# A diffusion layer on one core: first stage without GpSimd, DRAM sums filled later, modulations spread one by one, broadcasts moved up

## The chip, the cores and the metric

The kernel runs on one core of a Trainium2 chip. Times are microseconds (us) on the device. Five engines work side by side and meet through semaphores: TensorE (PE in the profile; its weight loads are PEld), VectorE (DVE), ScalarE (ACT), GpSimd (POOL) and SyncE (SP, which here only issues DMAs). ACT and POOL issue DMAs as well.

## The reference

One layer on 512 latent tokens x and 256 context tokens ctx, width 1024, all in float32. Nine modulation vectors come from c (for x) and from c_ctx (for ctx).

```python
h = h + 0.5 * g1 * swiglu(modulate(h, norm_ffn1, sh1, sc1), w_ffn1_in, w_ffn1_out)
hc = hc + 0.5 * g1c * swiglu(modulate(hc, norm_ffn1, sh1c, sc1c), w_ffn1_in, w_ffn1_out)
u, uc = modulate(h, norm_mix, sh2, sc2), modulate(hc, norm_mix, sh2c, sc2c)
kv_c = uc @ w_in[:, K0:G0]                       # the context gives only keys and values
q, k, v, rg, cv, ga, gb = split(u @ w_in)
o = bidir_retention(rope(q), rope(k), v, context states)
h = h + g2 * ((sigmoid(ga) * retention_out(o, rg) + sigmoid(gb) * conv_branch(cv)) @ w_out)
h = h + 0.5 * g3 * swiglu(modulate(h, norm_ffn2, sh3, sc3), w_ffn2_in, w_ffn2_out)
return rmsnorm(h, final_norm)

def modulate(x, w, shift, scale):
    return x * rsqrt(mean(x * x) + EPS) * w * (1 + scale) + shift
def swiglu(x, w_in, w_out):
    a, b = split(x @ w_in)
    return (silu(a) * b) @ w_out
# mods = split(silu(c) @ w_mod + b_mod, 9): sh1, sc1, g1, sh2, sc2, g2, sh3, sc3, g3
```

## The kernel before

Channels lie on the 128 partitions in eight blocks (KT = 8), tokens along the free dimension: 0 to 511 are x (`xs`), 512 to 767 ctx (`cx`). Each float32 operand is split into a high and a low part, `hi` (ScalarE, a rounding copy) and `lo` (VectorE, a subtraction), and each product is three matmuls (`mm3`: hi by hi, lo by hi, hi by lo). Weights come in units of 512 KB: a DMA on SP's queue into one of four `wraw` buffers, then `wh` on ScalarE and `wl` on VectorE.

The order of the instructions on each engine is made at build time by a list scheduler, from the program's order and from which buffers are free (6 `t`, 4 `sg`, 2 `wm`, 8 PSUM banks `ps`). At run time each engine goes through its list in order and waits at each instruction for what it needs. DMAs wait in the same way in the list of the engine that issues them.

- **First stage** (`start`, `first_mods`, `shift`, `norm_start`). x is loaded, its squares are summed over channels (`square_sum`, then `rstd_sum` with matmuls against ones), and 1/rms is broadcast over the partitions with one more matmul (`rstd_bcast`). For each block b, `first_mods` computes that block's scale and shift for x and ctx at once: the scale by eight small matmuls with `cs` (columns of silu(c), silu(c_ctx)), a copy of the two rows and a transpose; the shift by dots of the weight tile with the broadcast rows `ccrow`, for x on VectorE (L183), for ctx by a multiply on GpSimd (L186) and a sum on ScalarE (L187). `shift` adds the two halves and the bias (L194, L195). `norm_start` makes the block's operand (L530 to L533), and `products` runs the first two pairs of weight units of FFN1 on the blocks that are done. Then the context is done the same way, its matmuls after all products of x.
- **hdram** holds x and ctx in DRAM; FFN1's partial sums are added to it by accumulating DMAs (`part_sum`) and read back at the end.
- **FFN1** runs in six groups of hidden blocks; from the second on each block is a `chunk` (a seven-product scheme on four-block halves). The 56 other modulation tiles are loaded by GpSimd into `wm` (L200) and reduced by VectorE (L206), a few after each chunk or output pair (`mod_step(count)`).
- **Handover to the mixers** (`tail1`, `head2`, `retention(0)`, `keys_c`, `rotated`). FFN1's last outputs come in two halves of the tokens. Each half has its rstd sum, broadcast and norms; between them stand the context's keys. `rotated` makes keys and queries, `roped` turns them (L733 to L736), `strips` makes the decay tables with exp, `conv_at` a chunk of the convolution branch.

Of the kernel before, what the change touches and what calls it, by code (L numbers as in the profile page):

```python
# [54 lines left out]


# [6 lines left out]
def hybrid_layer_kernel(ctx: ExitStack, tc: tile.TileContext, a: dict, out: bass.AP):  # L63
# [62 lines left out]
    nc.sync.dma_start(cs, a["ccT"])  # L126
# [38 lines left out]
    rtags = [f"{t}{i}" for i in range(8) for t in ("th", "tl")]  # L165

    def first_mods(b):


        raw = [[t_((P, 512), F32, rtags[(4 * b + 2 * i + n) % 16]) for n in range(2)] for i in range(2)]  # L170
        for i in range(2):
            for n in range(2):
                nc.sync.dma_start(raw[i][n], a["w_mod0"][2 * b + i, :, n * 512:(n + 1) * 512])
        pm = ps()
        for k in range(KT):
            nc.tensor.matmul(pm[0:2, 0:P], cs[:, k, :], raw[0][k // 4][:, k % 4 * P:(k % 4 + 1) * P],
                             start=k == 0, stop=k == KT - 1)
        row = tmp()
        nc.vector.tensor_copy(row[0:2, 0:P], pm[0:2, 0:P])
        nc.tensor.transpose(pm[:, P:P + 2], row[0:2, 0:P], ident[0:2, 0:2])  # L180
        for n in range(2):
            c = slice(n * 512, (n + 1) * 512)
            nc.vector.scalar_tensor_tensor(tmp((P, 512), BF16), raw[1][n], 1.0, ccrow[0][:, c], ALU.mult, ALU.mult,  # L183
                                           accum_out=dots[:, b, 0, n:n + 1])
# [3 lines left out]
        nc.vector.tensor_scalar(ab1[:, 0, b, :], pm[:, P:P + 2], bm1[:, 8 + b:9 + b], vec[:, V_N1 + b:V_N1 + b + 1],  # L188
                                ALU.add, ALU.mult)
        shift(slice(b, b + 1), 0)  # L190

    def shift(bs, v):
        t = ab1[:, 1, bs, v]
        nc.vector.tensor_add(t, dots[:, bs, v, 0], dots[:, bs, v, 1])  # L194
        nc.vector.tensor_add(t, t, vec[:, V_BM + bs.start:V_BM + bs.stop])  # L195
# [183 lines left out]
    def chunk(j, u, t, keep):  # L379
# [34 lines left out]
        nc.scalar.activation(s[:, lo_], pa, AF.Silu)  # L414
        product(pd, w1, 1, [x[3] for x in t], False)
# [20 lines left out]
    def ffn1(u):  # L436
# [7 lines left out]
        def plain(pa, pb, pc):  # L444
            s = t_((P, LA), F32, "sg", 4)
            nc.scalar.activation(s[:, xs], pa, AF.Silu)
            nc.vector.tensor_mul(s[:, xs], s[:, xs], pb)
            nc.scalar.activation(s[:, cx], pc[:, 0, :], AF.Silu)
            nc.vector.tensor_mul(s[:, cx], s[:, cx], pc[:, 1, :])
            return s  # L450

        ux, uc = part(u, xs), part(u, cx)
        todo_g = [plain(*p) for p in start(ux, uc)]
# [4 lines left out]
        for gi, (k0, nk) in enumerate(GROUPS1):  # L458
            for j in range(2 if k0 == 0 else 0, nk):
                if k0 and j == nk - 1:  # L460
                    g.append((t_((P, LA), F32R, f"hx{2 * j}"), t_((P, LA), F32R, f"hx{2 * j + 1}")))
                    chunk(k0 + j, u, t, lambda s, c: split(g[-1][0][:, c], g[-1][1][:, c], s[:, c]))
                elif k0:
                    keep(j, chunk(k0 + j, u, t, None))
# [9 lines left out]
                keep(j, plain(pa, pb, pc))  # L474
# [9 lines left out]

            for mm in () if last else range(4):
                mod_step(STEPS_OUT[gi] * (mm + 1) // 4 - STEPS_OUT[gi] * mm // 4)
# [6 lines left out]
                for i in range(2):  # L493
                    part_sum(2 * mm + i, px[i], pc[i][:, :LC])
# [40 lines left out]
    def start(u, uc):  # L535
# [7 lines left out]
        r1 = r1c = None  # L543
# [8 lines left out]
        dg = rstd_sum(acc, sq, whole)  # L552
        for b in range(KT):
            first_mods(b)
            if b == 0:
                r1 = rstd_bcast(dg)
                w += units(a["w1i"][0])
# [3 lines left out]
            if b == 5:  # L561
                for i in range(KT):
                    nc.sync.dma_start(hx[i][:, cx], a["ctxT"][:, i, :])
# [5 lines left out]
        products(0, 7)  # L569
# [75 lines left out]
    def tail1(n, h, hc):  # L645
# [118 lines left out]
    def retention(hd):  # L764
# [35 lines left out]
        if hd == 0:  # L800
# [284 lines left out]
def _layout(x, c, ctx, c_ctx, w_mod, b_mod, norm_ffn1, w_ffn1_in, w_ffn1_out, norm_mix, w_in, ret_decay_f,  # L1085
# [15 lines left out]
    def out_groups(w, groups):  # L1101
# [3 lines left out]
    wn = w_mod[0][:, D:2 * D].reshape(KT, P, 8, P).transpose(2, 1, 0, 3).reshape(8, P, -1)  # L1105
# [16 lines left out]
        "w_mod0": np.stack([w for b in range(8) for w in (wn[b], wm[0, b])]),  # L1122
# [37 lines left out]
```

## Time and profile before

| | |
|---|---|
| median of three runs | 1781.86 us (1779.5 to 1781.98) |
| profiled execution | 1779.1 us |
| its span | 1777.0 us |
| mean granted TensorE clock | 0.985 |
| busy in the span: PE, DVE, ACT, POOL | 1723.9, 1150.4, 676.0, 141.6 us |

The span runs from the first to the last instruction that the profiler records; the execution's time adds what lies around it. "PE busy" counts matmuls at whatever clock was granted. In a row of waits, the first name is what stood still and the second what it waited for, by the line of each. In a row of the timeline the first number is the start in us, the second the length, and the bracket at the end the idle time before it with its releaser.

### The profile page before, as it was taken

How to read it: one execution, taken by the hardware profiler on the slowest of the kernel's cores; microseconds unless marked ns; L12 is line 12 of the kernel's file. 1: busy time of each engine (PE TensorE's matmuls, PEld its weight loads, DVE VectorE, ACT ScalarE, POOL GpSimd, SP SyncE). 2: the span in 40 equal slices, each digit the busy share in tenths (PEclk: the TensorE clock that was granted, in tenths of full speed). 3: DMA queues.
4: the chain of work that ended last, by engine and by line, in shares of the span. 5: the costliest groups of instructions: out<-in, count | busy, mean ns of one | idle time of the engine just before them, and what ended most of it. 6: DMA issues, size and time to landing. Idle time of an engine off the chain costs nothing.

```text
span 1777.0 us, 22523 instructions
## 1 busy us (share of the span) xinstructions
PE 1723.9 (97%) x8930; PEld 1498.8 (84%) x8930; DVE 1150.4 (65%) x1818; ACT 676.0 (38%) x969; POOL 141.6 (8%) x221
## 2 busy tenths in 40 slices
PE   5999999999999889999999999999999999999997
PEld 3689999989899878888888888888788988888887
DVE  5895868786677788793885679293765643333335
ACT  4644434434344522342342334233563432222222
POOL 3401020202112100010000000001100000000000
PEclk7999999999999999999999999999999999999999
DMA  9347373857665321142142115115552133222221
GB/s 347 110 143 154 120 182 109 196 177 195 201 171 177 109 83 60 69 157 72 52 156 87 55 69 176 60 48 177 191 196 100 60 119 95 100 95 99 98 84 48
DMA packets 68254, 221.97 MB, mean 125 GB/s; under 512 B 8178, under 2 KB 9202, under 8 KB 68148
## 3 DMA queue, kind: packets, MB, share of 16 engines
q1 hardware_dynamic: 45652, 146.84, 24.6%
q0 software_dynamic: 21920, 72.64, 14.6%
q8 instruction: 70, 1.15, 0.3%
q10 hardware_dynamic: 576, 1.05, 0.2%
q14 instruction: 36, 0.29, 0.0%
HBM read 192.18 MB, written 31.46 MB: 126 GB/s over the span
## 4 chain that ended last, share of the span: by engine, by line
PE 80%; issue 6%; DMA 6%; DVE 6%; ACT 1%; POOL 1%; SPq 0%; DVEq 0%; POOLq 0%; ACTq 0%
PE ps L112 23%; PE ps L113 23%; PE ps L111 23%; PE ps L404 9%; DMA wm<-in_w_mod 2%; DMA th<-in_w_mod 2%; DVE wl L104 1%; DVE h L716 1%; DMA wraw<-in_w_co 1%; DMA wraw<-in_w_v 0%; DMA kl<-in_dec 0%; POOL hdram L620 0%; DVE t L206 0%; DVE t L183 0%; PE ps L895 0%
## 5 line engine op out<-in xcount | busy, mean ns | idle before, releaser
L102 ACT CAST wh<-wraw 128x1024 fp32r<-128x1024 f32 (+2 forms) x212 | 219.5, 1037 | 559.9 <-PE ps L112 309.2
L104 DVE TENSOR_TENSOR wl<-wraw,wh 128x1024 fp32r<-128x1024 f32 (+2 forms) x212 | 254.4, 1203 | 198.3 <-ACT wh L102 193.5
L111 PE MATMUL ps<-uh,wh 128*128 128x512 f32 (+1 forms) x924 | 332.3, 362 | 1.5 <-ACT uh L292 1.1
L113 PE MATMUL ps<-uh,wl 128*128 128x512 f32 (+1 forms) x924 | 331.0, 359 | 0.0
L112 PE MATMUL ps<-ul,wh 128*128 128x512 f32 (+1 forms) x832 | 298.5, 360 | 0.2
L112 PE MATMUL ps<-gx,wh 128*128 128x512 f32 (+1 forms) x544 | 204.0, 377 | 0.0
L113 PE MATMUL ps<-gx,wl 128*128 128x512 f32 (+1 forms) x544 | 204.0, 377 | 0.0
L111 PE MATMUL ps<-gx,wh 128*128 128x512 f32 (+1 forms) x544 | 203.7, 377 | 0.2 <-ACT gx L300 0.2
L111 PEld LDWEIGHTS ps<-uh,wh 128*128 128x128 f32 x924 | 174.8, 190 | 28.2 <-ACT uh L292 1.5
L113 PEld LDWEIGHTS ps<-uh,wl 128*128 128x128 f32 x924 | 175.7, 190 | 25.4 <-issue 0.2
L716 DVE SCALAR_TENSOR_TENSOR h<-y,vec,h 128x512 f32<-128x512 f32 x240 | 179.7, 749 | 5.5
L112 PEld LDWEIGHTS ps<-ul,wh 128*128 128x128 f32 x832 | 158.4, 191 | 24.4 <-issue 0.9
L111 PE MATMUL ps<-hx,wh 128*128 128x512 f32 (+1 forms) x368 | 122.0, 335 | 7.4 <-ACT hx L300 7.4
L112 PE MATMUL ps<-hx,wh 128*128 128x512 f32 (+1 forms) x368 | 123.1, 335 | 0.0
L113 PE MATMUL ps<-hx,wl 128*128 128x512 f32 (+1 forms) x368 | 122.7, 334 | 0.0
L111 PEld LDWEIGHTS ps<-gx,wh 128*128 128x128 f32 x544 | 102.1, 188 | 19.2 <-ACT gx L300 0.4
L112 PEld LDWEIGHTS ps<-gx,wh 128*128 128x128 f32 x544 | 102.0, 188 | 18.7
L113 PEld LDWEIGHTS ps<-gx,wl 128*128 128x128 f32 x544 | 102.0, 188 | 18.7
L359 DVE TENSOR_TENSOR wl<-wraw,wh 128x1024 fp32r<-128x1024 f32 x54 | 66.1, 1224 | 54.5 <-ACT wh L358 54.2
L404 PE MATMUL ps<-th,wl 128*128 128x384 f32 x288 | 96.2, 334 | 0.0
L404 PE MATMUL ps<-th,wh 128*128 128x384 f32 x288 | 96.2, 334 | 0.0
L404 PE MATMUL ps<-tl,wh 128*128 128x384 f32 x288 | 96.2, 334 | 0.0
(277 smaller groups left out, 3109.4 us busy)
## 6 DMA issues: line engine op xcount, KB each, us to landing
wm<-in_w_mod POOLq DMA_DIRECT2D x56, 512.0 KB, 4.5
wraw<-in_w1i SPq DMA_DIRECT2D x44, 512.0 KB, 6.5
wraw<-in_w2i SPq DMA_DIRECT2D x44, 512.0 KB, 3.6
hdram<-sg POOLq DMA_DIRECT2D x40, 384.0 KB, 7.5
wraw<-in_w1o SPq DMA_DIRECT2D x16, 512.0 KB, 3.5
wraw<-in_w_cv SPq DMA_DIRECT2D x16, 512.0 KB, 4.3
wraw<-in_w_v SPq DMA_DIRECT2D x16, 512.0 KB, 6.0
wraw<-in_w_rg SPq DMA_DIRECT2D x16, 512.0 KB, 3.6
```

The lines of the kernel that those rows point to most:

```text
L102: nc.scalar.copy(hi, raw)
L104: nc.vector.tensor_sub(lo, raw, f32(hi))
L111: nc.tensor.matmul(o, w[0], x[0], start=first, stop=False)
L112: nc.tensor.matmul(o, w[0], x[1], start=False, stop=False)
L113: nc.tensor.matmul(o, w[1], x[0], start=False, stop=last)
L359: nc.vector.tensor_sub(lo, src, f32(hi))
L404: nc.tensor.matmul(o, w[i][:, ws], x[k][m], start=first and k == n == 0, stop=k == 3 and n == 2, skip_group_check=True)
L716: nc.vector.scalar_tensor_tensor(o, y[:, t:t + L], vec[:, w0 + t:w0 + t + 1], o, ALU.mult, ALU.add)
```

## The change

It has four parts.

1. **First stage.** For the first three blocks (`PE_SHIFT`) scale and shift of both x and ctx come from TensorE; w_mod0 is laid out for it on the host. For the other five, the dots of ctx are on VectorE too, inside the context's loop (`shift(b, 1)`). GpSimd's multiplies and ScalarE's sums are gone. `shift` is one instruction. The copy of the rows is on ScalarE. `load_mods` issues a block's loads one block earlier, with scales in `sg` or `wm` and shifts in `th`/`tl`. Products follow one block closer, all products of x come before the context's rstd, and the context's matmuls run block by block over four outputs. c's rows are loaded by ScalarE's queue.
2. **hdram** is filled after the first gate (a two-column DMA from the gate's tile makes it wait).
3. **Modulations**: one step at a time, in the middle and at the end of each chunk, and before each partial sum.
4. **Handover**: the first half's broadcast is called inside the context's keys, the second inside the first output of `rotated`, and the convolution's chunk before the strips.

```diff
+PE_SHIFT = 3
-    nc.sync.dma_start(cs, a["ccT"])
+    nc.scalar.dma_start(cs, a["ccT"])
...
+    def load_mods(b):
+        for i in range(2):
+            if i == 0 and b % 4 >= 2:
+                raw = t_((P, D), F32, "wm", 2)
+                nc.sync.dma_start(raw, a["w_mod0"][2 * b])
+                parts = [raw[:, :512], raw[:, 512:]]
+            else:
+                parts = [t_((P, 512), F32, "sg", 4) if i == 0 else t_((P, 512), F32, rtags[2 * b + n]) for n in range(2)]
+                for n in range(2):
+                    nc.sync.dma_start(parts[n], a["w_mod0"][2 * b + i, :, n * 512:(n + 1) * 512])
+            shifts[b, i] = parts
     def first_mods(b):
...
+        pm, row, n = ps(), tmp(), 2 if b < PE_SHIFT else 1
+        for i in range(n):
+            c, raw = slice(i * P, (i + 1) * P), shifts[b, i]
+            for k in range(KT):
+                nc.tensor.matmul(pm[0:2, c], cs[:, k, :], raw[k // 4][:, k % 4 * P:(k % 4 + 1) * P],
+                                 start=k == 0, stop=k == KT - 1)
+        nc.scalar.copy(row[0:2, :n * P], pm[0:2, :n * P])
...
-            m = tmp()
-            nc.gpsimd.tensor_mul(m, raw[1][n], ccrow[1][:, c])
-            nc.scalar.activation(m, m, AF.Copy, accum_out=dots[:, b, 1, n:n + 1])
...
+    def shift(b, v):
         for n in range(2):
...
+            nc.vector.scalar_tensor_tensor(tmp((P, 512), BF16), shifts[b, 1][n], 1.0, ccrow[v][:, c], ALU.mult,
+                                           ALU.mult, accum_out=dots[:, b, v, n:n + 1])
+        nc.vector.tensor_scalar(ab1[:, 1, b, v:v + 1], dots[:, b, v, 0:1], dots[:, b, v, 1:2],
+                                vec[:, V_BM + b:V_BM + b + 1], ALU.add, ALU.add)
...
+        nc.gpsimd.dma_start(hdram[:, 0, L - 1:L + 1], todo_g[0][:, L - 1:L + 1])
+        nc.gpsimd.dma_start(hdram[:, :, xs], a["xT"])
+        nc.gpsimd.dma_start(hdram[:, :, cx], a["ctxT"])
...
+            steps = spread(STEPS_IN[gi], 2 * nk - 1)
+            beside = lambda: mod_step(next(steps))
...
+                    keep(j, chunk(k0 + j, u, t, beside, None))
+                    beside()
                 if k0:
-                    mod_step(STEPS_IN[gi] * (j + 1) // nk - STEPS_IN[gi] * j // nk)
...
         for b in range(KT):
+            if b == 0:
+                w += units(a["w1i"][0])
+            if b + 1 < KT:
+                load_mods(b + 1)
             first_mods(b)
...
             if b >= 1:
-                products(0, b - 1)
+                products(0, b)
             if b >= 4:
-                products(1, b - 2)
+                products(1, b - 1)
...
-        dgc = rstd_sum(accc, sqc, wholec)
-        products(1, 7)
-        shift(slice(0, KT), 1)
-        r1c = rstd_bcast(dgc)
...
         products(0, KT)
         products(1, KT)
+        r1c = rstd_bcast(rstd_sum(accc, sqc, wholec))
+        s = [t_((P, LA), F32, "sg", 4) for _ in range(2)]
+        gate(s[0], xs, px[0], px[1])
+        pc = [ps()[:, :LC] for _ in range(4)]
+        for b in range(KT):
+            if b >= PE_SHIFT:
+                shift(b, 1)
+            norm_start(b, cx, r1c, deriv["c1"], *uc[b])
+            for i in range(4):
+                proj(pc[i], w[i], uc, (b,))
+        gate(s[1], xs, px[2], px[3])
+        for n in range(2):
+            gate(s[n], cx, pc[2 * n], pc[2 * n + 1])
         nc.gpsimd.dma_start(rope, a["rope"])
-        nc.gpsimd.dma_start(hdram[:, :, xs], a["xT"])
-        nc.gpsimd.dma_start(hdram[:, :, cx], a["ctxT"])
...
-        if n == 6:
-            st["ra"] = rstd_bcast(st["a"])
-        if n == 7:
-            norm_mods(h, st["ra"], deriv["x2"], st["u"], HALVES[0], range(4))
...
     def head2(n):
         if n == 0:
+            ra = rstd_bcast(st["a"])
+            norm_mods(h, ra, deriv["x2"], u, HALVES[0], range(4))
             st["b"] = rstd_sum(acc, st["sq", 256], HALVES[1])
...
-                proj(pc[:, i, :], wk[i], uc)
-                if hd == 0:
-                    head2(i)
+                for ks in (range(4), range(4, KT)):
+                    proj(pc[:, i, :], wk[i], uc, ks)
+                    if hd == i == ks[0] == 0:
+                        head2(0)
...
                 for i in range(len(w)):
                     proj(px[i][:, c], w[i], u, c=c)
-                if hook:
-                    hook()
-                    hook = None
+                    if hook:
+                        hook()
+                        hook = None
...
+            conv_at(hd)
             sx, sc = strips(hd)
-            conv_at(hd)
```

How the lists of the engines move, at the places that matter (line numbers of the changed kernel are larger: L255, L256, L269 became L269, L270, L283; L111 to L113 became L113 to L115; L206 became L220).

TensorE at the end of the first stage, before: the last of the context's rstd sum (`accc`), products of x (`uh`, `ul`, 128x512), and the context's broadcast (L269).

```order
L255 MATMUL ps_639<-ones,accc_129 128x2
L256 MATMUL ps_639<-ones,t_631 128x2
L112 MATMUL ps_183<-ul_33_144,wh_388 128x512
L113 MATMUL ps_183<-uh_32_143,wl_390 128x512
L111 MATMUL ps_180<-uh_34_145,wh_245 128x512
L112 MATMUL ps_180<-ul_35_146,wh_245 128x512
L113 MATMUL ps_180<-uh_34_145,wl_247 128x512
L111 MATMUL ps_181<-uh_34_145,wh_251 128x512
L112 MATMUL ps_181<-ul_35_146,wh_251 128x512
L113 MATMUL ps_181<-uh_34_145,wl_253 128x512
L269 MATMUL ps_669<-t_652,ones 128x256
L111 MATMUL ps_182<-uh_34_145,wh_382 128x512
```

The same place after:

```order
L114 MATMUL ps_183<-ul_35_146,wh_389 128x512
L115 MATMUL ps_183<-uh_34_145,wl_391 128x512
L269 MATMUL ps_622<-ones,accc_129 128x2
L270 MATMUL ps_622<-ones,t_602 128x2
L269 MATMUL ps_622<-ones,accc_129 128x2
L270 MATMUL ps_622<-ones,t_602 128x2
L283 MATMUL ps_638<-t_635,ones 128x256
L113 MATMUL ps_644<-uh_20_131,wh_218 128x256
L113 MATMUL ps_645<-uh_20_131,wh_224 128x256
```

The products of x are all done, and the broadcast follows its sum directly, with the context's matmuls (128x256) behind it.

GpSimd from the start, before (the copy to hdram, then modulation weights `wm`, then the multiplies of the first stage):

```order
L581 DMA rope<-in_rope 128x144
L582 DMA hdram<-in_xT 1024x512
L583 DMA hdram<-in_ctxT 1024x256
L200 DMA wm_1138<-in_w_mod 128x1024
L186 TENSOR_TENSOR t_230<-th_53_210,kl_85 128x512
L200 DMA wm_1146<-in_w_mod 128x1024
```

And after:

```order
L607 DMA rope<-in_rope 128x144
L214 DMA wm_1181<-in_w_mod 128x1024
L214 DMA wm_1193<-in_w_mod 128x1024
L466 DMA hdram<-sg_640 128x2
L467 DMA hdram<-in_xT 1024x512
L468 DMA hdram<-in_ctxT 1024x256
L214 DMA wm_1263<-in_w_mod 128x1024
```

The copy stands behind the first two modulation loads and waits for the gate's tile `sg`; the third modulation load stands behind it.

VectorE in FFN1, in the group in which TensorE waits at 393 us, before (L206 are modulations, L417 to L421 sums of a chunk):

```order
L104 TENSOR_TENSOR wl_3580<-wraw_3576,wh_3578 128x768
L104 TENSOR_TENSOR wl_3644<-wraw_3640,wh_3642 128x768
L206 SCALAR_TENSOR_TENSOR t_3574,mx<-wm_3572,kh_84 128x1024
L417 TENSOR_TENSOR t_3462<-t_3462,ps_3459 128x384
L206 SCALAR_TENSOR_TENSOR t_3632,mx<-wm_3630,kh_84 128x1024
L419 TENSOR_TENSOR t_3461<-t_3461,ps_3458 128x384
L230 TENSOR_TENSOR g_x_3634<-mx,vec 128x8
```

And after:

```order
L106 TENSOR_TENSOR wl_3561<-wraw_3557,wh_3559 128x768
L106 TENSOR_TENSOR wl_3619<-wraw_3615,wh_3617 128x768
L220 SCALAR_TENSOR_TENSOR t_3609,mx<-wm_3607,kh_84 128x1024
L432 TENSOR_TENSOR t_3447<-t_3447,ps_3444 128x384
L220 SCALAR_TENSOR_TENSOR t_3663,mx<-wm_3661,kh_84 128x1024
L434 TENSOR_TENSOR t_3446<-t_3446,ps_3443 128x384
L244 TENSOR_TENSOR g_x_3665<-mx,vec 128x8
```

The sequence there is the same.

TensorE at the handover, before: the last of the first half's rstd sum (`acc`), FFN1's last output, and the broadcast, with the context's keys behind it.

```order
L256 MATMUL ps_5451<-ones,t_5431 128x2
L113 MATMUL ps_5358<-hx_866_4744,wl_5090 128x256
L111 MATMUL ps_5358<-hx_891_4883,wh_5088 128x256
L112 MATMUL ps_5358<-hx_892_4884,wh_5088 128x256
L113 MATMUL ps_5358<-hx_891_4883,wl_5090 128x256
L111 MATMUL ps_5358<-hx_897_4895,wh_5088 128x256
L112 MATMUL ps_5358<-hx_898_4896,wh_5088 128x256
L113 MATMUL ps_5358<-hx_897_4895,wl_5090 128x256
L269 MATMUL ps_5501<-t_5464,ones 128x256
L111 MATMUL ps_5576<-uh_970_5279,wh_5566 128x256
```

And after, around the same broadcast:

```order
L113 MATMUL ps_5543<-uh_964_5264,wh_5539 128x256
L114 MATMUL ps_5543<-ul_965_5265,wh_5539 128x256
L115 MATMUL ps_5543<-uh_964_5264,wl_5541 128x256
L283 MATMUL ps_5556<-t_5449,ones 128x256
L113 MATMUL ps_5543<-uh_966_5266,wh_5539 128x256
```

It now stands inside the context's keys (`ps_5543` is the second key output's tile), 45 rows behind the last of its sum instead of 8. The second half's broadcast was 121 rows behind its sum, after all four outputs of the first half, and is now 25 rows behind it, after 12 matmuls of the first output. The first matmuls of retention on the turned keys (`gx` by `kh`) come 47 rows later in TensorE's list.

More of the change, by code (lines that the diff above doesn't have):

```diff
@@ L165, in hybrid_layer_kernel @@
     rtags = [f"{t}{i}" for i in range(8) for t in ("th", "tl")]
-    def first_mods(b):
[L170 to L173, printed above, removed]
-        pm = ps()
[L175 to L180, printed above, removed]
+    shifts = {}
@@ new lines, in first_mods @@
+    def first_mods(b):
+        pm, row, n = ps(), tmp(), 2 if b < PE_SHIFT else 1
[5 more added lines that the diff above has]
+        nc.scalar.copy(row[0:2, :n * P], pm[0:2, :n * P])
+        pm = ps()
+        for i in range(n):
+            nc.tensor.transpose(pm[:, 2 * i:2 * i + 2], row[0:2, i * P:(i + 1) * P], ident[0:2, 0:2])
+        nc.vector.tensor_scalar(ab1[:, 0, b, :], pm[:, 0:2], bm1[:, 8 + b:9 + b], vec[:, V_N1 + b:V_N1 + b + 1],
+                                ALU.add, ALU.mult)
+        if b < PE_SHIFT:
+            nc.vector.tensor_scalar_add(ab1[:, 1, b, :], pm[:, 2:4], vec[:, V_BM + b:V_BM + b + 1])
+        else:
+            shift(b, 0)
@@ L190, in first_mods @@
[L190 to L195, printed above, removed]
+            nc.vector.scalar_tensor_tensor(tmp((P, 512), BF16), shifts[b, 1][n], 1.0, ccrow[v][:, c], ALU.mult,
+                                           ALU.mult, accum_out=dots[:, b, v, n:n + 1])
+        nc.vector.tensor_scalar(ab1[:, 1, b, v:v + 1], dots[:, b, v, 0:1], dots[:, b, v, 1:2],
+                                vec[:, V_BM + b:V_BM + b + 1], ALU.add, ALU.add)
@@ L377, in operands, with chunk @@
         return out
-    def chunk(j, u, t, keep):
+    def chunk(j, u, t, beside, keep):
         r0, r1 = raw_tile((P, D)), raw_tile((P, D))
@@ L442, in keep, with gate @@
             g.append((hi, lo))
[L444 to L450, printed above, removed]
+        def gate(s, c, pa, pb):
+            nc.scalar.activation(s[:, c], pa, AF.Silu)
+            nc.vector.tensor_mul(s[:, c], s[:, c], pb)
         ux, uc = part(u, xs), part(u, cx)
-        todo_g = [plain(*p) for p in start(ux, uc)]
+        todo_g = start(ux, uc, gate)
+        nc.gpsimd.dma_start(hdram[:, 0, L - 1:L + 1], todo_g[0][:, L - 1:L + 1])
+        nc.gpsimd.dma_start(hdram[:, :, xs], a["xT"])
+        nc.gpsimd.dma_start(hdram[:, :, cx], a["ctxT"])
         t = [operands(kb) for kb in range(4)]
@@ L461, in ffn1 @@
                     g.append((t_((P, LA), F32R, f"hx{2 * j}"), t_((P, LA), F32R, f"hx{2 * j + 1}")))
[L462 removed]
+                    chunk(k0 + j, u, t, beside, lambda s, c: split(g[-1][0][:, c], g[-1][1][:, c], s[:, c]))
                 elif k0:
[L464 removed]
+                    keep(j, chunk(k0 + j, u, t, beside, None))
+                    beside()
                 if k0:
[L466 removed]
                     continue
@@ L473, in ffn1 @@
                 proj(pc[:, 1, :], wb, uc)
-                keep(j, plain(pa, pb, pc))
+                s = t_((P, LA), F32, "sg", 4)
+                gate(s, xs, pa, pb)
+                gate(s, cx, pc[:, 0, :], pc[:, 1, :])
+                keep(j, s)
             n = 2 * nk * P
@@ L533, in norm_start, with start @@
         nc.scalar.activation(src, v, AF.Identity, bias=sh)
-    def start(u, uc):
+    def start(u, uc, gate):
         for b in range(KT):
@@ L560, in start, with spread @@
                 w += units(a["w1i"][1])
-            if b == 5:
-                for i in range(KT):
-                    nc.sync.dma_start(hx[i][:, cx], a["ctxT"][:, i, :])
             if b >= 1:
-                products(0, b - 1)
+                products(0, b)
             if b >= 4:
-                products(1, b - 2)
+                products(1, b - 1)
+        for i in range(KT):
+            nc.sync.dma_start(hx[i][:, cx], a["ctxT"][:, i, :])
         sqc = [square_sum(accc, hx[j][:, cx], j) for j in range(KT)][-1]
-        products(0, 7)
-        dgc = rstd_sum(accc, sqc, wholec)
-        products(1, 7)
-        shift(slice(0, KT), 1)
-        r1c = rstd_bcast(dgc)
-        for b in range(KT):
-            norm_start(b, cx, r1c, deriv["c1"], *uc[b])
         products(0, KT)
         products(1, KT)
-        pc = [ps((P, 2, LC)) for _ in range(2)]
-        for i in range(4):
-            proj(pc[i // 2][:, i % 2, :], w[i], uc)
+        r1c = rstd_bcast(rstd_sum(accc, sqc, wholec))
[11 more added lines that the diff above has]
+            gate(s[n], cx, pc[2 * n], pc[2 * n + 1])
         nc.gpsimd.dma_start(rope, a["rope"])
-        nc.gpsimd.dma_start(hdram[:, :, xs], a["xT"])
-        nc.gpsimd.dma_start(hdram[:, :, cx], a["ctxT"])
-        return [(px[0], px[1], pc[0]), (px[2], px[3], pc[1])]
+        return s
     todo = list(range(len(MOD_STEPS)))
     hg = {key: cp.tile([P, 8], F32, name=f"g_{key}") for key in ("x1", "c1")}
+    def spread(total, slots):
+        return (total * (i + 1) // slots - total * i // slots for i in range(slots))
     def mod_step(count):
@@ L689, in head2 @@
         if n == 0:
+            ra = rstd_bcast(st["a"])
+            norm_mods(h, ra, deriv["x2"], u, HALVES[0], range(4))
             st["b"] = rstd_sum(acc, st["sq", 256], HALVES[1])
-            norm_mods(h, st["ra"], deriv["x2"], u, HALVES[0], range(4, KT))
+            norm_mods(h, ra, deriv["x2"], u, HALVES[0], range(4, KT))
         if n == 2:
@@ L1121, in _layout @@
         "vecs": np.concatenate(vecs, axis=1),
-        "w_mod0": np.stack([w for b in range(8) for w in (wn[b], wm[0, b])]),
+        "w_mod0": np.stack([w for b in range(8) for w in (wn[1, b], wn[0, b] if b < PE_SHIFT else wm[0, b])]),
         "w_mod": np.stack([wm[i, b] for i, b in MOD_STEPS]),
```

14 lines of the change are left out of this document (5 added, 9 removed).

## The prediction

> **What bounds the kernel now.** I read the page's totals and slices first, then what TensorE (PE) waited for, then the stretches of time with such waits.
>
> ```profile
> PE 1723.9 (97%) x8930; PEld 1498.8 (84%) x8930; DVE 1150.4 (65%) x1818; ACT 676.0 (38%) x969; POOL 141.6 (8%) x221
> PE   5999999999999889999999999999999999999997
> PEclk7999999999999999999999999999999999999999
> ```
>
> TensorE is busy 97% of the span of 1777.0 us, so only the missing 3% and the time at a low clock can be won without taking matmuls away. The missing share sits in the first slice (44 us, busy 5 tenths, clock 7) and in slices 14 and 15. The waits by cause (total us, times, longest):
>
> ```profile
> PE ps L255 <- DVE acc L246: 10.9, 1, 10.9
> PE ps L269 <- DVE t L262: 8.7, 3, 5.4
> PE ps L111 <- ACT hx L300: 7.4, 2, 3.8
> PE ps L159 <- ACT wraw L156: 5.9, 1, 5.9
> PE ps L180 <- DVE t L179: 5.8, 4, 2.5
> PE ps L111 <- ACT gx L300: 4.7, 2, 4.5
> PE ps L111 <- ACT uh L292: 1.1, 1, 1.1
> ```
>
> L255, L159 and L180 belong to the first stage. L269 (rstd broadcast; 5.4 of it at the handover), gx and uh belong to the handover from FFN1 to the mixers, and the two hx waits are inside FFN1. A wait costs more than itself, as the windows show (length, then busy us by engine, PEclk, DMA share, GB/s):
>
> ```profile
> 45.80:49.20 3.40, 1.58 (x10) 0.99 (x11) 3.40 (x10) 2.31 (x6) 1.21 (x1) 1.00 0.88 297
> 49.20:52.60 3.40, 3.40 (x15) 2.12 (x13) 3.40 (x6) 1.62 (x4) 3.26 (x2) 0.50 0.89 286
> 64.00:67.50 3.50, 2.38 (x11) 1.45 (x9) 2.86 (x8) 2.45 (x6) 1.59 (x1) 1.00 0.00 0
> 67.50:71.00 3.50, 2.93 (x21) 1.79 (x20) 2.71 (x6) 1.78 (x4) 1.66 (x2) 1.00 0.02 5
> 397.40:400.80 3.40, 3.35 (x9) 2.77 (x10) 2.61 (x6) 0.00 (x0) 0.53 (x1) 0.50 0.80 267
> 592.00:598.80 6.80, 4.12 (x17) 3.94 (x18) 6.56 (x18) 3.26 (x7) 0.00 (x0) 0.50 0.86 283
> 632.90:639.70 6.80, 5.38 (x17) 4.49 (x18) 6.72 (x10) 1.25 (x2) 0.00 (x0) 0.50 0.15 52
> ```
>
> A stretch in which TensorE works 1.58 of 3.4 us is followed by 3.4 us at a granted clock of 0.50; one with 2.38 of 3.5 us is not. At half clock half of the busy time is lost: 1.7 us after an FFN1 wait, 4.12/2 = 2.1 and 5.38/2 = 2.7 at the handover.
>
> **First stage.** All its loads share the DMA engines with a copy of x and ctx to DRAM (hdram), issued at the very start by GpSimd (POOL), which the change puts behind the context's gate.
>
> ```profile
> 12.00:24.00 12.00, 1.09 (x5) 0.64 (x4) 4.06 (x6) 6.35 (x10) 0.00 (x0) 0.63 1.03 394
> 88.00:100.00 12.00, 12.00 (x79) 11.00 (x79) 11.99 (x20) 9.26 (x12) 0.00 (x0) 1.00 0.29 89
> hdram<-in_xT POOLq DMA_DIRECT2D x1, 2048.0 KB, 12.1
> hdram<-in_ctxT POOLq DMA_DIRECT2D x1, 1024.0 KB, 15.6
> 23.36 0.59 PE L255 MATMUL ps<-ones,acc 128*128 128x2 f32 x2 [10.91 <-DVE acc L246]
> 48.70 0.37 SPq L173 DMA_DIRECT2D tl<-in_w_mod  x1
> tl<-in_w_mod SPq DMA_DIRECT2D x16, 256.0 KB, 6.6
> ```
>
> From 12 to 24 us the DMA engines are full at 394 GB/s. The copy is 3.1 MB, 8.0 us at that rate. Out of the way, the sum of squares can start at 15.4 instead of 23.36, and the last modulation weights (issued at 48.70, landing 6.6 us later) arrive at 47 instead of 55. Where the copy goes, the DMA engines are 0.29 busy: hidden. The rows of c and c_ctx go to ScalarE's queue (the first thing on it, so nothing waits behind them); SP is then free earlier for x. Scales and shifts get other buffers; no load waits longer by the order of the queues.
>
> ```profile
> L183 DVE SCALAR_TENSOR_TENSOR t<-tl,kh 128x512 bf16<-128x512 f32 x8 | 6.5, 814 | 0.0
> L183 DVE SCALAR_TENSOR_TENSOR t<-th,kh 128x512 bf16<-128x512 f32 x8 | 5.8, 728 | 0.0
> L194 DVE TENSOR_TENSOR ab<-dots 128x1 f32<-128x1 f32 x8 | 6.8, 849 | 0.0
> L194 DVE TENSOR_TENSOR ab<-dots 128x8 f32<-128x8 f32 x1 | 0.2, 167 | 0.0
> L195 DVE TENSOR_TENSOR ab<-ab,vec 128x1 f32<-128x1 f32 x8 | 5.3, 665 | 0.0
> L176 PE MATMUL ps<-tl,cs 128*2 128x128 f32 x64 | 10.4, 309 | 0.0
> L176 PE MATMUL ps<-th,cs 128*2 128x128 f32 x64 | 9.7, 302 | 0.0
> ```
>
> VectorE (DVE) is busy all the time in this stage (3.40 of 3.40 in both windows from 45.8 to 52.6), while TensorE is not. The change takes off it: the row copy, which goes to ScalarE (left uncounted); two adds for one (8 x (0.85 + 0.67 - 0.17) = 10.8; an add over one column takes 0.85 with GpSimd's multiplies running and 0.17 over eight columns without, so I take most of it for waiting on GpSimd); and three blocks' dots (3 x 1.54 = 4.6). That is 15.4 us of its work. TensorE gets those three blocks' shifts: 20.1/8 = 2.5 us each, 7.5 in all, while it waits for weights. GpSimd's 16 multiplies and ScalarE's 16 sums go; neither was last.
>
> The x products, which ended at 81.6 (below), are now bounded by TensorE: from 15.4, 11 rounds of 2.5 us for modulations = 27.5, and 96 products at 0.26 (seven matmuls in 79.74 to 81.59 below) = 25: 68; by loads 47 + one block's chain and two blocks' products, about 60. I take 64. Then comes what I hold to be the cost of the change:
>
> ```profile
> 76.91 0.38 PE L255 MATMUL ps<-ones,accc 128*128 128x2 f32 x2
> 79.74 0.63 PE L269 MATMUL ps<-t,ones 128*128 128x256 f32 x2
> 81.59 0.40 PE L111 MATMUL ps<-uh,wh 128*128 128x256 f32 x2
> 94.19 0.40 PE L111 MATMUL ps<-uh,wh 128*128 128x512 f32 x1
> L530 DVE SCALAR_TENSOR_TENSOR t<-hx,ab,ps 128x256 f32<-128x256 f32 x8 | 3.6, 476 | 0.8 <-PE ps L269 0.8
> L532 DVE SCALAR_TENSOR_TENSOR ul<-t,ab,uh 128x256 fp32r<-128x256 f32 x8 | 3.8, 481 | 0.1
> L104 DVE TENSOR_TENSOR wl<-wraw,wh 128x1024 fp32r<-128x1024 f32 x6 | 7.3, 1214 | 0.0
> ```
>
> In before the context's rstd sum (76.91) and broadcast (79.74) stand among x products. In the new order nothing stands between them, and the gates' Silu and products go first on ScalarE and VectorE: TensorE waits 2.8 us at least; with two table changes and two gates, up to 6.5; I take 4.5. The context products, 12.6 us of TensorE (81.59 to 94.19), now wait block by block for VectorE: 8 x (0.48 + 0.48) for the norms, ten dots at 0.77, five small adds at 0.17: 16.2 us, 1 us until the first. Stage end: 64 + 4.5 + 1 + 16.2 = 85.7, against 94.2: 8.5 earlier. Share 12.6/16.2 = 0.78 busy is above the 2.38 of 3.5 that kept the clock, but the broadcast wait is long enough for one half-clock window, 1.7. The third weight unit's lo halves (two of 1.2 us) queue on VectorE behind this: 3 us. First stage: 8.5 - 1.7 - 3 = 3.8 gained; ends: 8 gained (no wait for the lo halves), 5 lost (products at 68, wait 6.5, two half-clock windows more).
>
> The Trainium skill, "TensorE: Matmul & The Clock Gate", Part 1, gives the cold state after at least one idle window of about 3.4 us. The trace is stricter (the window of 1.58 us busy cost a cold one). By the page, the broadcast wait would cost no clock and the sum would be 1.7 lower.
>
> **FFN1's modulations one at a time: nothing.** In front of the two FFN1 waits, VectorE's instructions stand in the same sequence as before; the change in program order is undone by the scheduler. What starts these waits remains:
>
> ```profile
> 390.26 1.23 DVE L206 SCALAR_TENSOR_TENSOR t<-wm,kh 128x1024 bf16<-128x1024 f32 x1 [3.93 <-DMA wm<-in_w_mod]
> ```
>
> VectorE stands 3.9 us before a modulation whose weights are still on their way, and chunk sums and operand splits are queued behind it. GpSimd issues one such load a place earlier elsewhere; I price that at 0, with ends of 10.8 us gained (two waits, 7.4, and two half windows, 3.4) and 3 lost (one more such wait).
>
> **Handover.** The first-half broadcast moves from 8 rows behind its rstd sum to 45 rows behind it. With 96 context matmuls in 12.6 us, 0.13 each, that is 5.9 us of cover for a wait of 5.4, and the exp strips leave the chain on ScalarE and VectorE: the wait goes. The second broadcast moves ahead, to 12 matmuls into the rotated outputs, so the uh wait (1.1) goes, and RoPE's operands are wanted 47 rows later behind convolution projections, so the gx wait (4.5) goes. Idle 5.4 + 1.1 + 4.5 = 11.0, clock 2.1 + 2.7 = 4.8: 15.8 at most. What is late next is the second broadcast: 24 matmuls, 3.1 us, stand between it and its sum, where a chain of 2.8 us (76.91 to 79.74) shares VectorE with four norms (4 x 0.96 = 3.8): a wait of up to 3.5, I take 3.0. Gain 12.8; ends 6 (RoPE still late: 4.5 and its 2.7 stay, and 2.6 of the new wait) and 15.8. The strips and their loads move behind the convolution's first projections; their results are wanted only by retention.
>
> **Sum.** The profiled execution took 1779.1 us, 2.1 over its span. 1779.1 - 3.8 - 0 - 12.8 = 1762.5. The median of the runs, 1781.86, is 2.8 above that execution: 1765.3, rounded up to 1766.
>
> **The rivals.**
> - FFN1's waits go as well: 10.8 more, about 1755. For it: that is what the code is written for. Against: the sequence on VectorE. 0.13.
> - The first stage loses 5 instead of gaining 4: 1775. For it: nothing covers the context's broadcast. Against: 15.4 us less on VectorE and loads 8 us earlier. 0.14.
> - The handover's waits only move (RoPE on VectorE still last): gain 6, 1773. Against: 47 rows of cover. 0.12.
> - Slower: the late copy. It starts at about 86 to 90, and the next modulation weights stand behind it on GpSimd's queue. If it lands 15.6 us later, it is out at 106; in before these loads were issued only from 112.84 us on:
>
> ```profile
> 112.84 0.60 POOL L200 DMA_DIRECT2D wm<-in_w_mod  x1 [43.68 <-DVE t L206]
> ```
>
> Each us past about 113 delays the first gate vector, then the partial sums, whose PSUM buffers TensorE needs. It would decide from about 17 us on, with the copy landing at 130: over 1785. Against: the copy is 8 us at the full rate, the engines there are 0.29 busy. 0.05. The Trainium skill, "DMA: Bandwidth & Descriptors", Queues, rings and completion order, says that each DMA engine takes the queue rows with work in turn, packet by packet. By that the copy would also halve the rate of SP's loads while it lasts; no run here shows how much slack they have.
> - Gains cancelled, no change: 0.05. The forecast holds the other 0.51.
>
> **Numbers.** A difference of 0.2%, 3.6 us, is what can be told from none. The forecast's own range is 1758 to 1772. With the rivals, 1753 (FFN1's waits gone, most of the start's gain) to 1777 (first stage lost, small handover gain). Faster: all but the last two and a few hundredths for two losses together: 0.88; same 0.06; slower 0.06.
>
> **What would show it.** PE starts L255's successor at about 15, x products end near 64, a wait of 3 to 6 us stands at the context's broadcast, and waits of under 1 us recur in its blocks; the stage ends some 4 us earlier than before by the 300th matmul. The two FFN1 waits on hx stay at 3 to 4 us. At the handover one wait of 2 to 3 us before the second broadcast is left, and the granted clock stays 1.0 but for one window. The prediction is wrong if the first stage's new waits bring half-clock windows through the whole context stage, if the hx waits vanish, or if RoPE still holds TensorE.

## The result: 1767.4 us against 1780.7 us, and the profile after

The changed kernel takes 1767.38 us (median of four runs, 1765.94 to 1770.89), the kernel before 1780.68 (1776.28 to 1781.98). The ratio is 0.9937, with a 95% interval of 0.9914 to 0.9959. The profiled execution took 1767.34 us, its span 1765.6, 11.4 less than before.

What TensorE waited for in the changed kernel (total us, times, longest); L269, L283, L113 stand for L255, L269, L111:

```profile
PE ps L283 <- DVE t L276: 7.7, 4, 2.4
PE ps L113 <- ACT hx L314: 6.7, 2, 3.9
PE ps L161 <- DVE ident_h L145: 6.4, 1, 6.4
PE ps L113 <- ACT wh L104: 3.3, 2, 2.9
PE ps L269 <- DVE acc L260: 1.6, 1, 1.6
PE ps L113 <- ACT uh L552: 1.1, 1, 1.1
```

The first rstd sum's wait fell from 10.9 to 1.6, the one on the handover's first broadcast (5.4) is gone, and of those on gx (4.7) 0.2 is left. New are the broadcast in the context's stage (in the first row) and the third weight unit (wh). The hx waits inside FFN1 stand.

TensorE's starts at the ends of the first stage, from its timeline, each with the idle time before it:

```profile
14.28 0.38 PE L269 MATMUL ps<-ones,acc 128*128 128x2 f32 x2 [1.64 <-DVE acc L260]
67.96 0.28 PE L269 MATMUL ps<-ones,accc 128*128 128x2 f32 x2
71.07 0.70 PE L283 MATMUL ps<-t,ones 128*128 128x256 f32 x2 [2.17 <-DVE t L276]
72.89 0.52 PE L113 MATMUL ps<-uh,wh 128*128 128x256 f32 x1 [1.11 <-ACT uh L552]
90.40 0.80 PE L113 MATMUL ps<-uh,wh 128*128 128x512 f32 x1 [2.89 <-ACT wh L104]
```

And windows of the same stage and of the handover (length, busy us by engine, PEclk, DMA share, GB/s):

```profile
20.00:40.00 20.00, 19.10 (x129) 12.45 (x128) 9.81 (x23) 7.23 (x12) 0.00 (x0) 0.96 0.75 274
40.00:60.00 20.00, 19.82 (x109) 13.56 (x108) 11.71 (x30) 6.30 (x12) 0.53 (x1) 1.00 0.68 226
73.00:76.40 3.40, 3.40 (x16) 3.40 (x17) 3.40 (x11) 2.05 (x6) 0.00 (x0) 0.50 0.02 5
90.00:96.80 6.80, 5.94 (x14) 4.36 (x15) 6.80 (x11) 6.30 (x8) 1.93 (x3) 0.50 0.49 170
602.00:605.40 3.40, 3.22 (x16) 3.03 (x15) 3.09 (x9) 3.17 (x8) 0.00 (x0) 0.51 0.06 8
```

TensorE, not VectorE, now sets the pace from 20 to 60 us. The x products end at 68 instead of 81. By the first matmul of the third unit the lead is 94.19 - 90.40 = 3.8 us, and 6.8 us at half clock follow that wait. To follow the lead further I count the matmuls of the projections (L111 to L113 before, L113 to L115 after; 7092 in both) and compare when the same one starts. At the 300th the lead is gone (113.4 before, 113.2 after; the 1000th: 401.6 and 400.7; the 2000th, behind the handover: 693.8 and 683.1). So the profiled gain lies at the handover. The experiments ask whether the first stage really contributes nothing.

### The profile page after: what moved, and what is told of

It is laid out like the page before. It is cut to its first block, busy times and chain, and to the rows that moved or that the text cites. A ratio compares the mean times of both kernels' runs of the same rounds, so it can differ in the third digit from the quotient of the medians.

```text
span 1765.6 us, 22548 instructions
## 1 busy us (share of the span) xinstructions
PE 1727.5 (98%) x8981; PEld 1502.5 (85%) x8981; DVE 1140.4 (65%) x1813; ACT 670.3 (38%) x946; POOL 114.9 (7%) x206
## 5 line engine op out<-in xcount | busy, mean ns | idle before, releaser
L113 PE MATMUL ps<-uh,wh 128*128 128x512 f32 (+1 forms) x924 | 332.5, 364 | 5.2 <-ACT wh L104 3.3
L115 PE MATMUL ps<-uh,wl 128*128 128x512 f32 (+1 forms) x924 | 331.1, 360 | 0.7 <-DVE wl L106 0.7
L115 PE MATMUL ps<-gx,wl 128*128 128x512 f32 (+1 forms) x544 | 204.0, 377 | 0.0
L113 PE MATMUL ps<-gx,wh 128*128 128x512 f32 (+1 forms) x544 | 203.7, 378 | 0.2 <-ACT gx L314 0.2
L113 PEld LDWEIGHTS ps<-uh,wh 128*128 128x128 f32 x924 | 175.1, 191 | 33.7 <-ACT wh L104 4.3
L115 PEld LDWEIGHTS ps<-uh,wl 128*128 128x128 f32 x924 | 176.0, 191 | 26.5 <-DVE wl L106 1.1
L113 PE MATMUL ps<-hx,wh 128*128 128x512 f32 (+1 forms) x368 | 121.4, 333 | 6.7 <-ACT hx L314 6.7
L115 PE MATMUL ps<-hx,wl 128*128 128x512 f32 (+1 forms) x368 | 123.5, 336 | 0.0
L113 PEld LDWEIGHTS ps<-gx,wh 128*128 128x128 f32 x544 | 102.1, 188 | 19.1 <-ACT gx L314 0.4
L115 PEld LDWEIGHTS ps<-gx,wl 128*128 128x128 f32 x544 | 102.0, 188 | 18.8
```

The lines of the kernel that those rows point to most:

```text
L113: nc.tensor.matmul(o, w[0], x[0], start=first, stop=False)
L115: nc.tensor.matmul(o, w[1], x[0], start=False, stop=last)
```

## The experiments

All are compared with the kernel before on the same chip (median 1778 to 1780 us). Lines shift a little from kernel to kernel.

**The handover alone.** The kernel before, with only the edits of `tail1`, `head2`, `keys_c`, `rotated` and the order of `conv_at` and `strips`:

```diff
-            st["ra"] = rstd_bcast(st["a"])            # in tail1
...
+            ra = rstd_bcast(st["a"])                  # in head2(0)
...
+                    if hd == i == ks[0] == 0:
+                        head2(0)                      # after four of the first key's eight blocks
...
+            conv_at(hd)
             sx, sc = strips(hd)
-            conv_at(hd)
```

> The kernel before with the handover part of the change alone (first and second broadcast moved, convolution ahead of the strips). Theory A (the handover carries nearly the whole gain of 13 us; the first stage nets nothing): 1770 us, 10 to 11 us under before; the waits on t L262, uh and gx fall from 11.0 us to about 3.5 and one half-clock window is left there. Theory B (the gain is shared, the first stage and the modulations bring half): 1774 us.

1769.42 us against 1778.17, ratio 0.9944 (0.9927 to 0.9961). Before and then this run from 580 to 660 us:

```profile
580.00:660.00 80.00, 68.91 (x452) 63.38 (x451) 59.34 (x117) 33.48 (x55) 3.76 (x7) 0.91 0.29 95
580.00:660.00 80.00, 76.13 (x513) 69.90 (x512) 69.86 (x132) 36.92 (x58) 4.86 (x9) 1.00 0.33 109
```

TensorE is busy 7.2 us more of the same 80, at a full clock. Theory A: the handover alone gives 0.56% where the whole change gives 0.63%, so nearly all of it (8.8 us here, 13.3 in the comparison above, whose kernel before stood at 1780.7). Which of the handover's three edits carries how much was not run.

**The late copy alone.** The kernel before, with the copy to hdram behind the first gate:

```diff
-        nc.gpsimd.dma_start(hdram[:, :, xs], a["xT"])    # in start
-        nc.gpsimd.dma_start(hdram[:, :, cx], a["ctxT"])
...
+        nc.gpsimd.dma_start(hdram[:, 0, L - 1:L + 1], todo_g[0][:, L - 1:L + 1])   # behind the gates
+        nc.gpsimd.dma_start(hdram[:, :, xs], a["xT"])
+        nc.gpsimd.dma_start(hdram[:, :, cx], a["ctxT"])
```

> The kernel before with only the copy to hdram moved behind the first gate; the first stage keeps GpSimd's multiplies and its order. Theory A (the late copy is worth about 8 us, and the rearranged first stage of the changed kernel gives them back): 1772 us, the 300th projection matmul at about 105 us instead of 113. Theory B (VectorE sets the pace of the stage up to 112 us, so earlier loads bring nothing): 1780 us, the 300th matmul at 112 to 113.

1771.77 against 1778.17, 0.996 (0.9945 to 0.9975). Its rstd sum and the first matmul of the third unit:

```profile
16.30 0.59 PE L255 MATMUL ps<-ones,acc 128*128 128x2 f32 x2 [4.97 <-DVE acc L246]
87.18 0.40 PE L111 MATMUL ps<-uh,wh 128*128 128x512 f32 x1
```

23.36 became 16.30 and 94.19 became 87.18, and the 300th projection matmul comes at 106.4: 7.0 us, kept. So the old first stage with the late copy is 6.8 us ahead of the changed one at that matmul. The rearrangement gave the copy's gain back.

**The copy early again**, in the changed kernel (the same edit backwards):

> The changed kernel with only the copy to hdram put back to the start. Theory A: the first stage loses the 8 us that the late copy gave, so 1775 us, some 8 us over the changed kernel, first rstd sum at about 22 us instead of 14.3. Theory B (the first stage is bounded by TensorE and VectorE from 30 us on): 1767 to 1769.

1775.96, 0.9987 (0.9975 to 0.9999). The sum starts at 20.09, the third unit at 97.95:

```profile
20.09 0.58 PE L269 MATMUL ps<-ones,acc 128*128 128x2 f32 x2 [6.89 <-DVE acc L260]
97.95 0.80 PE L113 MATMUL ps<-uh,wh 128*128 128x512 f32 x1 [2.88 <-ACT wh L104]
```

With its copy early the rearranged stage ends 3.8 us after that of before (94.19), and the kernel loses most of its gain. Both runs put the copy at 6 to 9 us.

**The modulations as before**, in the changed kernel:

```diff
-                    beside()
                 if k0:
+                    mod_step(STEPS_IN[gi] * (j + 1) // nk - STEPS_IN[gi] * j // nk)
...
```

> The changed kernel with the modulations again issued as before (a few after each chunk and output pair). Theory A (the scheduler undoes the order, the spreading is worth nothing): 1767 us, within 2 us of the changed kernel, two waits of 3 to 4 us on hx. Theory B (spreading took 1 us off a wait and off its clock): 1769 to 1771.

1765.97, 0.9928 (0.9912 to 0.9944), against 0.9937 with the spreading: no difference that these runs can tell. The hx waits are 2.8 and 4.0, as in the changed kernel. So no gain of the spreading is shown.

**Late copy and handover**, added to the kernel before:

> The kernel before with the late copy and the new handover together, its first stage and modulations otherwise as before. Theory A (the two gains lie apart and add up): 8.7 + 6.4 = 15 us under before, about 1763 us against 1778 for before in the last comparison, 3 to 5 us under the changed kernel. Theory B (a gain at the start is lost again in FFN1 or at the handover): 1767 to 1769.

1760.83 against 1778.34, 0.9904 (0.9887 to 0.9921). The product of the two single ratios is 0.996 x 0.9944 = 0.9904: they add up. This is 5.9 us (0.3%) better than the changed kernel by the ratios, with the first stage otherwise left alone.

**What the rearranged stage loses**, in three steps on the changed kernel. First, cover the broadcast:

```diff
-        ...                                              # load the context, sum its squares
+            if b == 6:
+                ...                                      # the same, before the last block of x
+        dgc = rstd_sum(accc, sqc, wholec)
         products(0, KT)
+        r1c = rstd_bcast(dgc)
         products(1, KT)
-        r1c = rstd_bcast(rstd_sum(accc, sqc, wholec))
```

> The changed kernel with the context loaded and squared before the last block of x and its rstd sum placed ahead of the last products of x, so that products cover the broadcast. Theory A (the uncovered broadcast cost 2.2 + 1.1 us and a half-clock window): those two waits go, 3 us less than the changed kernel, about 1764 us. Theory B (VectorE's dots bound the context's stage, so TensorE only waits later): within 1 us of the changed kernel.

1767.17, 0.993 (0.9911 to 0.9949): no better than the changed kernel. Yet of the waits of 2.2 and 1.1 only 0.2 is left, and the 300th matmul comes at 108.1 instead of 113.2. The trace shows where most of these 5 us went: at about 1265 us, where the mixers' branches are merged, TensorE waits for another broadcast (this run, then the changed kernel):

```profile
1264.02 2.08 PE L283 MATMUL ps<-t,ones 128*128 128x512 f32 x2 [3.45 <-DVE t L276]
1266.82 1.12 PE L283 MATMUL ps<-t,ones 128*128 128x512 f32 x2 [1.42 <-DVE t L276]
```

The wait is 2.0 us longer, and 6.8 us at half clock follow it (5.48 of them busy, so 2.7 lost) where the changed kernel had none. That wait differs from run to run of these kernels (0.2 to 3.5 us); why, the runs don't settle. So the total alone would have hidden what this step gained.

Second, the context's dots go into the loop over x:

```diff
         else:
             shift(b, 0)
+            shift(b, 1)
...
-            if b >= PE_SHIFT:
-                shift(b, 1)
```

> As the run before it, and the context's ten dots made in the loop over x, where VectorE has time. Theory A (dots on VectorE, 8 us, make TensorE wait in the context's stage, 16.2 against 12.6 us): some 2 us less than without; the wait of 2.9 us on the third weight unit stays, and its half-clock windows with it. Theory B (the stage's end is set by that weight unit alone): the same as the run before it.

1762.31, 0.9909 (0.9891 to 0.9926). The 300th matmul is at 105.7, 2.4 earlier than without. The wait on the third unit did not stay at 2.9, as I had expected: it was already 1.5 us in the step before and is 1.3 now.

Third, outputs 2 and 3 run three blocks late, so that the first two units' buffers come free:

```diff
-            for i in range(4):
+            for i in range(2):
+                proj(pc[i], w[i], uc, (b,))
+            if b >= 3:
+                for i in range(2, 4):
+                    proj(pc[i], w[i], uc, (b - 3,))
+        for b in range(5, KT):
+            for i in range(2, 4):
                 proj(pc[i], w[i], uc, (b,))
```

> As the run before it, and the context's outputs 2 and 3 three blocks behind outputs 0 and 1, so that the first two weight units' buffers come free before the stage ends. Theory A (the third unit waits because all four units are held until the context's last block): the 2.9 us wait and its half-clock windows go, the 300th projection matmul comes at about 104 us, 1757 to 1760 us. Theory B (its hi and lo halves are late on ScalarE and VectorE whatever the buffers): the wait stays, 1763.

1760.01, 0.9898 (0.9881 to 0.9915). The third unit starts without a wait:

```profile
84.42 0.28 PE L115 MATMUL ps<-uh,wl 128*128 128x256 f32 x1
84.53 0.40 PE L113 MATMUL ps<-uh,wh 128*128 128x512 f32 x1
```

The 300th matmul is at 103.7 us: 9.4 earlier than in the changed kernel. The steps gave 5.0, 2.4 and 2.0, so the rearranged stage lost by all three: the uncovered broadcast, VectorE's dots, and weight buffers held to the end. Repaired, it is 2.6 us ahead of the old stage with the late copy.

**Other numbers of modulations per group**, on that version, first 4, 4, 4, 4 and then 6, 6, 2, 2 instead of 2, 2, 6, 6:

```diff
-STEPS_IN = (0, 2, 2, 6, 6, 8)
+STEPS_IN = (0, 4, 4, 4, 4, 8)
```

> The run with cover, early dots and lag, with the modulations of FFN1's chunks spread evenly over the groups: 4, 4, 4, 4 instead of 2, 2, 6, 6 (the last group keeps 8). Theory A (the two waits on hx come from VectorE standing before a modulation whose load GpSimd issued too late, in the two groups with 6): both waits shrink to under 1.5 us and their half-clock windows go, 5 to 10 us less, about 1752 us. Theory B (the same wait comes with the last chunk of any group, since the list scheduler gathers modulations there): the hx waits stay, or move to the groups that now have 4; within 3 us.

> The same with 6, 6, 2, 2. Theory A: no wait on hx is left in the two groups with 2; in the groups of four chunks, 6 steps are 1.5 a chunk and cause a wait of at most 2 us: 1753 us. Theory B: the waits move to the first two groups in full, 1760 us.

1753.78, 0.9849 (0.9833 to 0.9865), and 1762.32, 0.9908 (0.9888 to 0.9927). The waits on hx of the two:

```profile
PE ps L113 <- ACT hx L315: 7.2, 2, 3.6
PE ps L113 <- ACT hx L315: 8.1, 3, 3.5
```

Theory B held on the waits of the first: they stay, at 3.6 us. With 6, 6, 2, 2 neither theory held: the two waits stay where they were (3.5 and 3.3), though their groups have only 2 modulations, and a third of 1.3 us joins them. The first is the fastest kernel of the study all the same, though not for the reason expected: at the late broadcast it waits 0.23 us where its base waits 1.98, and no half-clock window follows there or at the handover. That the new numbers of modulations bring this about is not shown. Its base, then it, at the late broadcast and at the handover:

```profile
1258.19 1.74 PE L284 MATMUL ps<-t,ones 128*128 128x512 f32 x2 [1.98 <-DVE t L277]
1254.56 1.13 PE L284 MATMUL ps<-t,ones 128*128 128x512 f32 x2 [0.23 <-DVE t L277]
589.60:596.40 6.80, 5.29 (x23) 5.11 (x23) 6.53 (x19) 6.07 (x11) 0.00 (x0) 0.50 0.14 39
589.00:595.80 6.80, 4.40 (x33) 4.15 (x34) 6.07 (x19) 6.05 (x11) 0.00 (x0) 1.00 0.19 76
```

**Modulations held back**, to settle what the hx waits are. On the version with 4, 4, 4, 4, the last chunk of groups 4 and 5 has no modulation, and loads behind it wait for that chunk's split. The part on the loads:

```diff
...
+        if after is not None:
+            nc.gpsimd.tensor_copy(raw[:, 0:1], after)
         nc.gpsimd.dma_start(raw, a["w_mod"][n])
...
```

> The run with 4, 4, 4, 4, in whose groups 4 and 5 no modulation stands between the last chunk's sums and its operand split on VectorE: the last chunk has none, and the loads of those after it wait for that split (GpSimd writes one column of the buffer from it first). Theory A (VectorE standing before a modulation whose load is late holds back the split): both waits of 3.6 us on hx and their half-clock windows go, 8 to 10 us less, 1744 to 1747 us. Theory B (the split is late by itself, behind TensorE's last products and ScalarE): waits of 2 us or more stay, 1752 to 1754. Theory C (the held modulations then come too late for the partial sums): a new wait in the output pairs, no gain.

1767.61, 0.9932 (0.9918 to 0.9946): slower than its base. Its waits (total us, times, longest), on TensorE and then on VectorE from 380 to 430 us:

```profile
PE ps L421 <- DVE t L435: 10.2, 2, 5.5
DVE t L223 <- DMA wm<-in_w_mod: 19.7, 7, 5.0
```

No wait on hx is left, and the 1000th matmul comes 5.6 us earlier than in its base: the modulations in front of the split did cause it. But VectorE now stands before the held loads a group later, and TensorE waits 5.5 and 4.7 us for chunk sums there, with 13.7 us of half clock. Of Theory C this much held: the wait has moved, and it has grown; it stands at chunk sums, not in the output pairs.

**No multiplies on GpSimd**, in the kernel before. The run leaves out the products of c_ctx with the first shift's weights, that is GpSimd's 16 multiplies and ScalarE's 16 sums of them:

```diff
-            m = tmp()
-            nc.gpsimd.tensor_mul(m, raw[1][n], ccrow[1][:, c])
-            nc.scalar.activation(m, m, AF.Copy, accum_out=dots[:, b, 1, n:n + 1])
```

> The kernel before without GpSimd's 16 multiplies and ScalarE's 16 sums (the context's first shift lacks its weight term). Theory A (VectorE's small adds of 0.85 and 0.67 us wait for the SBUF port that GpSimd's multiplies hold): they fall to 0.2 us, the multiplies cost the first stage its pace on VectorE, and the x products end some 6 us earlier (75 instead of 81.6); the 300th projection matmul comes 2 to 6 us earlier, about 1775 us. Theory B (the adds are slow in themselves, or wait for ScalarE's sums): they stay at 0.6 us or more when nothing runs on GpSimd, or the stage's end does not move since the loads bound it: 1778 us.

1771.91 against 1780.26, 0.9955 (0.9941 to 0.9969). Groups by line from 24 to 95 us (busy, mean ns, idle before), L192 and L193 being L194 and L195 of before, and the first context matmul and third unit:

```profile
L193 DVE TENSOR_TENSOR ab<-ab,vec 128x1 f32<-128x1 f32 x8 | 1.2, 152 | 0.0
L192 DVE TENSOR_TENSOR ab<-dots 128x1 f32<-128x1 f32 x8 | 1.1, 142 | 0.0
73.26 0.40 PE L111 MATMUL ps<-uh,wh 128*128 128x256 f32 x2
85.85 0.40 PE L111 MATMUL ps<-uh,wh 128*128 128x512 f32 x1
```

The adds fall from 849 and 665 ns to 142 and 152, which is 9.8 us less on VectorE, and the x products end 8.3 us earlier although the loads are as before (first rstd sum at 23.73). Multiplies and sums together were as large a cost as the copy. This run takes both away at once; which of the two slowed the adds, the trace of the kernel before shows:

```profile
44.50 1.29 POOL L186 TENSOR_TENSOR t<-th,kl 128x512 f32<-128x512 f32 x1 [2.07 <-ACT t L187]
44.70 1.10 DVE L194 TENSOR_TENSOR ab<-dots 128x1 f32<-128x1 f32 x1
49.23 0.14 DVE L194 TENSOR_TENSOR ab<-dots 128x1 f32<-128x1 f32 x1
49.34 2.29 POOL L186 TENSOR_TENSOR t<-th,kl 128x512 f32<-128x512 f32 x1 [2.33 <-DVE ab L188]
```

The first add ends with the multiply beside it (45.80 and 45.79); the second falls between two multiplies and takes 0.14. So it is with all 16: twelve take 0.64 to 1.24 us and end within 0.03 us of the end of a multiply, four meet none and take 0.14 or 0.15. It is the multiplies. The changed kernel has this gain and the late copy's; no run has these two without the rest, so what they give together stays open.

## Why the prediction was right

Forecast 1766, measured 1767.38. The handover was named as the main gain, and it was. That the number is so near is in part luck. For the profiled execution I forecast 16.6 us less (1779.1 to 1762.5), and it became 11.8 less (1767.34): 3.6 too much in the first stage and 3.0 at the handover, less what FFN1 and the rest gained. Of these 4.8 us too much, 3.5 were covered by the 2.8 that I added because the median before lay above its profiled execution, and by rounding up; after, the median and the profiled execution are the same. Step by step:

- **Loads and first rstd sum**: 15.4 forecast, 14.28 measured. The late copy alone gives 16.30; the rest goes with the other edits of the loads, which without the late copy start the sum at 20.09 instead of 23.36. The copy was issued at 92 us and had landed by 106, and the next modulation load behind it was issued at 113.05 (112.84 before), waiting for VectorE. The late-copy rival did not come.
- **End of the x products**: 64 forecast, 68 measured. Of my two bounds, TensorE's (68) was the one that held, not the mean with the loads' (60): it was busy 19.8 of 20 us. I mis-sized this term by 4.
- **The context's broadcast**: 4.5 + 1 = 5.5 us forecast from the last x product to the context's first matmul, 4.9 measured (67.96 to 72.89), of which 2.17 and 1.11 are waits. The gates' Silu and the first table change (65.31 to 66.59) ran under the last products, the second (68.09 to 69.37) did not.
- **The context's matmuls**: 16.2 forecast, and 1.7 for a half-clock window; 14.6 measured (72.89 to 87.5) with that window in it (73.0 to 76.4). Mis-sized by 3.3. VectorE was busy all 14.6 us, as forecast, but a block with dots took it 2.2 us (77.86 to 80.05), where I had added up 0.96 + 1.54 + 0.17 = 2.67: in the trace each instruction starts just before the one ahead of it ends.
- **The third unit's wait**: 3 forecast, 2.89 measured. The experiments name its cause better than I did: held buffers as well as late halves.
- **The stage's end**: 94.2 - 3.8 = 90.4 forecast, 90.40 measured. That it fits is luck: +4.0, -0.6, -3.3 and -0.1 cancel.
- **Clock**: I counted one window, at the broadcast (it is in the 14.6 above). The wait on the third unit had its own 6.8 us at half clock, 5.94/2 = 3.0 lost, which I left out, and a second wait of 0.46 behind it. With them the first stage's 3.8 gained became 0.2 at the 300th matmul, where I had said some 4. This is the step that failed within the right total.
- **FFN1**: 0 forecast; 0.7 gained between the 300th and the 1000th matmul, hx 7.4 before, 6.7 after. The run with the old modulations has the same waits.
- **Handover**: 12.8 forecast, 9.8 between the 1000th and the 2000th matmul, and 8.8 in the run alone. The broadcast, uh and gx waits went as forecast, the wait before the second broadcast was 2.4 for 3.0. What I missed: small waits on uh and wl (0.6 and 0.7 in all), and the second broadcast's half-clock window (602 to 605.4, 3.22/2 = 1.6 lost), which I named among the signs but left out of the sum.

The Trainium skill, "TensorE: Matmul & The Clock Gate", Part 1, would by its idle window have left out the 1.7 at the broadcast; the trace does not agree: the waits of 2.17 and 1.11, both under a window, were followed by the window at 0.50 from 73.0.

What I got wrong in the reading is the shape of the first stage: I took the rearrangement and the late copy as one sum. They are two, of 6 to 9 gained and about 7 given back.

## What to carry to other kernels

Price each part of a joint change alone: a rearrangement that shows as "a little gain" can hide a larger one that another part pays for. When work is moved off an engine, look at what stood there as cover (here x products between a sum and its broadcast) and at which buffers the new order holds to the end. Where an engine works its list in order and stands before a late transfer, holding the transfer back takes the wait away there and brings it where the transfer is next wanted (two waits of 3.6 us became 5.5 and 4.7).

## What the runs showed of the hardware that I had not expected

- A GpSimd multiply of two 128x512 tiles slowed VectorE's adds of one column four- to sixfold (849 to 142 and 665 to 152 ns without it): an add that met a multiply ended with it. The 16 of them, with ScalarE's sums, cost 8 us of the stage. The Trainium skill, "SBUF — State Buffer", SBUF: two separate sides, has it as an exclusive lock on a port pair that both engines share, taken for a whole instruction, by VectorE's operations with two inputs in SBUF among others; by that rule the adds should fall to their own length without GpSimd, and they do.
- The same kind of wait can cost no half-clock time, 3.4 us or 6.8 us of it. The second broadcast's wait of 2.39 us at the handover was followed by 3.4 us in the changed kernel, by 6.8 in its form with the early copy, by none in the handover alone. So two kernels can differ by 3 us for waits that are alike. In each of the 14 traces all changes of the granted clock lie whole multiples of 3.413 us apart, and where this grid stands against the span's start differs from trace to trace. A stretch of it at full clock in which TensorE was busy less than 0.43 of the time was always followed by half clock, one over 0.65 never after the first 20 us; between the two both came, so how a wait falls on the grid seems to decide, which no run tests.
